# adaLN projections of a two-layer backbone: row tiles summed on VectorE, the rows of a tile on TensorE

## The chip, the cores and the metric

The kernel runs on one core of a Trainium2 chip. The metric is the device time of one execution in microseconds (us), lower is better. The engines named below are TensorE (PE in the views; PEld is its weight load), VectorE (DVE), ScalarE (ACT), GpSimd (POOL) and SyncE (SP), whose queue issues the large loads in order.

## The reference

A backbone of two layers with 1024 features works on 512 tokens: 256 of a context and 256 latents. Each layer has a mixer (attention, a Fourier branch and a recurrence, gated and merged) and an FFN with a convolution. Both are modulated by six chunks of 1024 columns, a product of a conditioning vector with `w_ada` and a bias: one vector for the latents, one for the context.

```python
silu_c = jax.nn.silu(c)
silu_cc = jax.nn.silu(c_ctx)
for l in range(DEPTH):
    mx = jnp.split((silu_c @ w_ada[l] + b_ada[l])[:, None, :], N_MOD, axis=-1)
    mc = jnp.split(silu_cc @ w_ada[l] + b_ada[l], N_MOD, axis=-1)
    hx = modulate(rms_norm(x, norm_mix[l]), mx[0], mx[1])
    hc = modulate(rms_norm(ctx, norm_mix[l]), mc[0], mc[1])
    ...
    x = x + mx[2] * y_x
    x = x + mx[5] * conv_ffn(modulate(rms_norm(x, norm_ffn[l]), mx[3], mx[4]), ...)
    if not last:
        ...
        ctx = ctx + mc[2] * y_c
        ctx = ctx + mc[5] * conv_ffn(modulate(rms_norm(ctx, norm_ffn[l]), mc[3], mc[4]), ...)
```

`w_ada` has 1024 rows and 6144 columns per layer, 24 MB in fp32. The last layer's context is read by its attention, so chunks 0 and 1 are needed there for both streams; chunks 2 to 5 only for the latents.

## The kernel before

Tokens lie feature-major. Every large product is split in three fp32r matmuls (`gemm`, recorded at L129): high times high, high times low, low times high. Weights come in loads of up to 1 MB: `chunk` (L164) issues them on SyncE into one of three `raw` buffers. A unit of weights is then split: `wh` is a rounded copy (L151 on ScalarE, or L153 on VectorE where `wmode["hi"]` says so, as in both layers' branches) and `wl` the rest (L158 on VectorE). There are three `wh` and three `wl` buffers. A usual load feeds two units, a unit feeds 24 matmuls.

The program runs through: a start with the first adaLN block in quarters (`ada_quarter`), layer 0's attention (70 to 176 us), its branches and output (to 512), its FFN (to 890), layer 1's attention (to 1004) and branches (to 1147), and the rest of layer 1. These are rough bounds, read from the trace.

The other five adaLN blocks, of two chunks each (2048 columns), are made by `ada_steps`. A step loads 128 rows of a block and multiplies: the stationary operand is `cvec`, 128 rows by 32 columns of which two hold the two conditioning vectors, the moving one 512 columns of weights. Four such matmuls fill four strips of 32 partitions of one bank, `pa`, and eight steps add up in it. Then VectorE copies the bank out (`adar`, L361), four transposes (`pt`, L364) bring the features onto partitions, and two adds (L368) put the bias on.

`ada_steps` is a generator whose steps are put between other work: `emit` takes so many steps at once, `spread` takes a fraction of a step with each later load of weights. Layer 0's blocks 1 and 2 go at two steps per head into its attention, layer 1's block 0 into layer 0's FFN, layer 1's blocks 1 and 2 into its attention (one step per head) and branches. A scheduler orders each engine's instructions from there; loads keep the program's order.

The fp32 `pa` matmuls have two records each in the trace. Tiles are named in the views: `sc`, `pt` (L832) and `pv` are the attention's scores, transposes and weighted values, `pr` its probabilities, `proj`, `gt`, `out`, `down` the large products, `uf`, `fa`, `ff` the Fourier features, `y`, `sg`, `ri` and `av` tiles of the recurrence and the merge.

## Time and profile before

| | |
|---|---|
| runs | 1417.83, 1414.15, 1417.03 us, median 1417.03 |
| span of the profiled execution | 1416.0 us |
| TensorE busy | 1374.2 us (97%) |
| VectorE busy | 892.9 us (63%) |
| ScalarE busy | 668.8 us (47%) |
| GpSimd busy | 231.9 us (16%) |
| read from HBM | 193.02 MB, 137 GB/s over the span |

The profile is of one execution. Its span runs from the first to the last instruction, and the runs' median stands 1.0 us above it. Busy shares are means over the whole span; the stretches differ, and the windows below tell them apart. The chain that ended last is followed back from the last instruction, at each step to what released it.

### The profile page before, as it was taken

To read this page: it belongs to the slowest core of one execution; us is meant where nothing else is said; L and a number is where in the kernel's file an instruction comes from. 1 tells how busy PE (TensorE), PEld (TensorE's weight loads), DVE (VectorE), ACT (ScalarE), POOL (GpSimd) and SP (SyncE) were. 2 spreads that over 40 slices of the span, in tenths; PEclk is the share of its full clock that TensorE was granted. 3 is DMA by queue.
4 is the path that set the end of the run, shared out by engine and by line. 5 is a ranking of instruction groups with operands and counts; after the bars stand their busy time and mean duration, and the time that the engine had idled before them with its cause. 6 is when DMAs were issued, how large, how long until landed. Compare 5 with 4: busy or idle time off the path is not lost.

```text
span 1416.0 us, 20938 instructions
## 1 busy us (share of the span) xinstructions
PE 1374.2 (97%) x8362; PEld 1172.5 (83%) x8362; DVE 892.9 (63%) x1451; ACT 668.8 (47%) x1136; POOL 231.9 (16%) x223
## 2 busy tenths in 40 slices
PE   7999999999999999999999999999999999999997
PEld 5676598888888898888888887878688899999997
DVE  3687648667634565555443543687788986777575
ACT  5575635423532444344322433475355665566454
POOL 2021013113200101211100111010122431122012
PEclk9999999999999999999999999999999999999999
DMA  9433715233233502222343337225465666455643
GB/s 332 135 107 131 272 35 170 80 97 100 79 100 110 172 31 90 86 96 87 89 123 120 104 116 245 62 80 191 152 219 183 197 190 199 135 194 175 196 140 100
DMA packets 187777, 195.41 MB, mean 138 GB/s; under 512 B 9340, under 2 KB 178290, under 8 KB 182560
## 3 DMA queue, kind: packets, MB, share of 16 engines
q1 hardware_dynamic: 186624, 193.23, 42.6%
q8 instruction: 65, 1.06, 0.3%
q0 software_dynamic: 1056, 0.86, 0.2%
q14 instruction: 32, 0.26, 0.1%
HBM read 193.02 MB, written 1.05 MB: 137 GB/s over the span
## 4 chain that ended last, share of the span: by engine, by line
PE 85%; DVE 7%; DMA 3%; ACT 2%; issue 2%; SPq 0%; POOL 0%; ACTq 0%; DVEq 0%; POOLq 0%
PE proj L129 49%; PE down L129 8%; PE out L129 7%; PE lat L129 4%; PE pa L129 3%; PE uf L129 2%; PE sc L129 2%; PE pv L129 2%; PE gt L129 2%; DVE wl L158 2%; PE pt L832 1%; DVE wh L153 1%; DMA raw<-in_w_in_dram 1%; DMA raw<-in_w_ada_dram 1%; PE kn L129 1%
## 5 line engine op out<-in xcount | busy, mean ns | idle before, releaser
L158 DVE TENSOR_TENSOR wl<-raw,wh 128x1024 fp32r<-128x1024 f32 (+9 forms) x339 | 339.4, 1014 | 160.8 <-ACT wh L151 156.1
L129 PE MATMUL proj<-hh,wh 128*128 128x512 f32 (+1 forms) x1232 | 417.8, 340 | 5.5 <-DVE sg L989 2.2
L129 PE MATMUL proj<-hh,wl 128*128 128x512 f32 (+1 forms) x1232 | 416.9, 339 | 0.2 <-DVE wl L158 0.2
L129 PE MATMUL proj<-hl,wh 128*128 128x512 f32 (+1 forms) x1232 | 416.8, 339 | 0.0
L151 ACT CAST wh<-raw 128x1024 fp32r<-128x1024 f32 (+7 forms) x275 | 216.3, 808 | 264.0 <-PE proj L129 153.9
L129 PEld LDWEIGHTS proj<-hh,wh 128*128 128x128 f32 x1232 | 236.1, 192 | 31.9 <-issue 3.1
L129 PEld LDWEIGHTS proj<-hh,wl 128*128 128x128 f32 x1232 | 236.1, 192 | 25.3 <-DVE wl L158 0.7
L129 PEld LDWEIGHTS proj<-hl,wh 128*128 128x128 f32 x1232 | 236.0, 192 | 24.5
L1181 POOL TENSOR_TENSOR gate<-gate,up 128x512 f32<-128x512 f32 (+1 forms) x44 | 55.3, 1257 | 445.4 <-ACT gate L1180 424.7
L153 DVE CAST wh<-raw 128x1024 fp32r<-128x1024 f32 x64 | 54.4, 853 | 52.7 <-PE proj L129 46.4
L129 PE MATMUL down<-gTh,wh 128*128 128x512 f32 (+1 forms) x224 | 75.5, 337 | 0.0
L129 PE MATMUL down<-gTh,wl 128*128 128x512 f32 (+1 forms) x224 | 75.4, 337 | 0.0
L129 PE MATMUL down<-gTl,wh 128*128 128x512 f32 (+1 forms) x224 | 75.3, 336 | 0.0
L158 DVE TENSOR_TENSOR gTl<-gate,gTh 128x512 fp32r<-128x512 f32 (+1 forms) x44 | 24.6, 559 | 78.5 <-ACT gTh L151 78.5
L129 PE MATMUL pa<-raw,cvec 128*32 128x512 f32 (+1 forms) x576 | 62.7, 457 | 3.9 <-DMA raw<-in_w_ada_dram 3.8
L442 POOL TENSOR_TENSOR sq<-sq,sq 128x256 f32<-128x256 f32 (+1 forms) x28 | 31.6, 1129 | 198.6 <-ACT sq L440 197.0
L1070 DVE SCALAR_TENSOR_TENSOR xr<-out,ada,xr 128x256 f32<-128x256 f32 x48 | 22.2, 480 | 44.1 <-PE out L129 44.1
L129 PE MATMUL out<-mh,wl 128*128 128x256 f32 (+1 forms) x152 | 47.4, 312 | 0.0
L129 PE MATMUL out<-mh,wh 128*128 128x256 f32 (+1 forms) x152 | 47.4, 313 | 0.0
L129 PE MATMUL out<-ml,wh 128*128 128x256 f32 (+1 forms) x152 | 47.4, 312 | 0.0
L151 ACT CAST gTh<-gate 128x512 fp32r<-128x512 f32 (+1 forms) x44 | 22.6, 514 | 51.3 <-POOL gate L1181 51.3
L129 PEld LDWEIGHTS down<-gTh,wh 128*128 128x128 f32 x224 | 42.5, 190 | 4.4
(287 smaller groups left out, 2725.3 us busy)
## 6 DMA issues: line engine op xcount, KB each, us to landing
raw<-in_w_up_dram SPq DMA_DIRECT2D x44, 1024.0 KB, 5.0
raw<-in_w_ada_dram SPq DMA_DIRECT2D x40, 1024.0 KB, 4.9
raw<-in_w_in_dram SPq DMA_DIRECT2D x30, 1024.0 KB, 5.3
raw<-in_w_down_dram SPq DMA_DIRECT2D x16, 896.0 KB, 5.2
raw<-in_w_ada_dram SPq DMA_DIRECT2D x32, 256.0 KB, 7.5
raw<-in_w_in_dram SPq DMA_DIRECT2D x16, 512.0 KB, 4.9
raw<-in_w_out_dram SPq DMA_DIRECT2D x8, 1024.0 KB, 5.3
raw<-in_w_down_dram SPq DMA_DIRECT2D x16, 512.0 KB, 3.8
```

Of the source, the lines that this page charges most:

```text
L129: pinned(nc.tensor.matmul(o, lhsT, rhs, start=start, stop=stop))
L151: nc.scalar.copy(out, in_)
L153: eng.tensor_copy(out, in_)
L158: (lo_eng or nc.vector).tensor_tensor(lo, src, hi, op=ALU.subtract)
L442: eng.tensor_tensor(self.terms[0][:, r], self.terms[0][:, r], sq[:, r], op=ALU.add)
L832: nc.tensor.transpose(o[:, c], probs[i][:, kt * P : (kt + 1) * P], ident)
L1070: nc.vector.scalar_tensor_tensor(xr[m][:, r], o[:, y], gate[:, s, m : m + 1], xr[m][:, r], op0=ALU.mult, op1=ALU.add)
L1181: nc.gpsimd.tensor_tensor(g, g, us[z], op=ALU.mult)
```

## The change

The five blocks are cut into 16 jobs. A job loads half tiles of 512 rows by 512 columns (1 MB, four row tiles of 128). VectorE multiplies each row tile by its 128 values of the conditioning vector, a scalar per partition, and adds it to an accumulator 128x512: one TENSOR_SCALAR and seven SCALAR_TENSOR_TENSOR for each of two accumulators. TensorE then sums over the 128 partitions with a stationary block of ones, four strips of 256 columns; ScalarE copies the sums (`adar`), two transposes and four small adds follow. `ada_both` is a job of 512 columns for both streams (two loads), `ada_latent` one of 1024 columns for the latents alone (four loads). Layer 0 has eight `ada_both`; layer 1 has four, and four `ada_latent` for chunks 2 to 5, whose context columns are filled with zeros. There are 40 loads of 1 MB as before.

Where they stand changes too. Layer 0's attention takes one step per pair of heads, its branches the rest of layer 0's jobs, layer 0's FFN all of layer 1's; layer 1's mixer has none. In layer 0's branches the `wh` copies go from VectorE to ScalarE. The accumulators share slots with other tiles, but have two buffers each of their own in layer 0's FFN. Of the diff, removed comments and the end of the old `ada_steps` are left out:

```diff
-    def ada_steps(l, blk, col, res, tag="raw"):
-        pa = bank("pa", "e")
-        for k in range(8):
-            v = chunk(a["w_ada"][l][k * P : (k + 1) * P, blk * 2048 : (blk + 1) * 2048].unsqueeze(1), 1, 2048, tag)
-            for j in range(4):
-                mm(pa[32 * j : 32 * j + 32, :], cvec[:, k, :], v[:, 0, 512 * j : 512 * (j + 1)], k == 0, k == 7)
-            if k < 7:
+    def ada_steps(l, jobs):
+
+        cols = columns_of[l]
+
+        def fetch(job, i):
+            c0, half = job[0][i]
+            src = a["w_ada"][l][half * 512 : (half + 1) * 512, c0 : c0 + 512]
+            return chunk(src.rearrange("(k p) c -> p k c", p=P), 4, 512)
+
+        def summed(quarters, two):
+            pa = bank("pa", "e")
+            for g, (z, o, *_) in enumerate(quarters):
+                mm(pa[32 * g : 32 * g + 32, 0:256], ones[:, 0:32], two[z][:, o : o + 256], True, True)
+            rows = slot("adar", "s", F32)
+            nc.scalar.copy(rows[:, 0:256], pa[:, 0:256])
+            return quarters, pa, rows
+
+        def spread_out(quarters, pa, rows):
+            for u in range(2):
+                nc.tensor.transpose(pa[:, 256 + u * P : 256 + (u + 1) * P], rows[:, u * P : (u + 1) * P], ident)
+            view = pa[:, 256:512].rearrange("p (u r) -> p r u", u=2)
+            for g, (z, o, s, j) in enumerate(quarters):
+                blk, f = j // 16, j % 16
+                nc.vector.tensor_tensor(
+                    adas[l][blk][:, s, f : f + 2], view[:, 32 * g], cols["b_ada"][:, j : j + 2], op=ALU.add
+                )
+
+        sums = None
+        for n, job in enumerate(jobs):
+            halves, quarters, todo = job
+            v = fetch(job, 0)
+            yield
+            if sums:
+                spread_out(*sums)
+            accs = [slot("acc", t, F32) for t in ("aa", "ab")]
+            for i, (c0, half) in enumerate(halves):
+                after = fetch(job, i + 1) if i + 1 < len(halves) else None
+                for k in range(4):
+                    for z, s in todo[i]:
+                        w, sc = v[:, k, :], cvec[:, 4 * half + k, s : s + 1]
+                        if half == 0 and k == 0:
+                            nc.vector.tensor_scalar(accs[z], w, sc, None, op0=ALU.mult)
+                        else:
+                            nc.vector.scalar_tensor_tensor(accs[z], w, sc, accs[z], op0=ALU.mult, op1=ALU.add)
+                    if k == 1 and len(todo[i]) > 1:
+                        yield
+                v = after
                 yield
-        rows = slot("adar", "s", F32)
-        nc.vector.tensor_copy(rows, pa)
...
+            sums = summed(quarters, accs)
+        yield
+        spread_out(*sums)
         yield
+    def ada_both(chunk_of, part):
+
+        c0 = chunk_of * D + part * 512
+        quarters = [(s, o, s, (c0 + o) // P) for s in range(2) for o in (0, 256)]
+        return ((c0, 0), (c0, 1)), quarters, [[(0, 0), (1, 1)]] * 2
+
+    def ada_latent(chunk_of):
+
+        c0 = chunk_of * D
+        quarters = [(z, o, 1, (c0 + z * 512 + o) // P) for z in range(2) for o in (0, 256)]
+        return (
+            tuple((c0 + z * 512, half) for z in range(2) for half in range(2)),
+            quarters,
+            [[(z, 1)] for z in range(2) for _ in range(2)],
+        )
...
-                    emit(steps, 1 if last else 2)
+                    if not last and e == 1:
+                        emit(steps, 1)
...
-                    wmode["hi"] = [nc.vector]
-                    if last:
-                        spread(steps, 0.5)
+                    wmode["hi"] = [nc.vector] if last else [nc.scalar]
+                    if not last:
+                        emit(steps, 1)
+                        spread(steps, 1.6)
...
-            spread(steps, 0.4)
+            spread(steps, 1.6)
...
-        with phase("ffn", gT=32, c=8), banks(dict(out="mm"), mm=5, rb=2):
+        with phase("ffn", gT=32, c=8, **({} if last else dict(aa=2, ab=2))), banks(dict(out="mm"), mm=5, rb=2):
...
+    for b in range(1, 3):
+        nc.gpsimd.memset(adas[1][b], 0.0)
+    parts_of = lambda chunks: [ada_both(c, part) for c in chunks for part in range(2)]
...
-        0, columns_of[0], adas[0], False, h, first_tiles, chain(par0, ada(0, 1), ada(0, 2)), sq_ffn,
+        0, columns_of[0], adas[0], False, h, first_tiles, chain(par0, ada_steps(0, parts_of((2, 3, 4, 5)))), sq_ffn,
...
-    steps = chain(iter([None] * 3), params(1, nc.gpsimd), final_gains(), ada(1, 0))
+    steps = chain(
+        params(1, nc.gpsimd), final_gains(),
+        ada_steps(1, parts_of((0, 1)) + [ada_latent(c) for c in range(2, 6)]),
+    )
...
-    steps_mix = chain(ada(1, 1), ada(1, 2))
...
-        1, columns_of[1], adas[1], True, h_mix, lambda half: None, steps_mix, sq_ffn,
+        1, columns_of[1], adas[1], True, h_mix, lambda half: None, iter(()), sq_ffn,
```

On TensorE, in layer 0's attention before, a chunk's four matmuls stand between the attention's own (`pv` weighted values, `pt` transposes, `sc` scores):

```order
L129 MATMUL pv_1889<-ptl_1867,vh_1379 64x256
L129 MATMUL pv_1889<-pth_1866,vl_1380 64x256
L129 MATMUL pa_1830<-raw_1943,cvec 32x512
L832 MATMUL pt_1920<-ident,pr_1843 128x128
L832 MATMUL pt_1920<-ident,pr_1855 128x128
L832 MATMUL pt_1920<-ident,pr_1843 128x128
L832 MATMUL pt_1920<-ident,pr_1855 128x128
...
L129 MATMUL pv_1889<-ptl_1876,vh_1399 64x256
L129 MATMUL pv_1889<-pth_1875,vl_1400 64x256
L129 MATMUL pa_1830<-raw_1943,cvec 32x512 x3
L129 MATMUL pa_1830<-raw_1949,cvec 32x512 x4
L129 MATMUL sc_1955<-kh_779,qh_1687 128x256
```

In the changed kernel, at the end of the first job there:

```order
L129 MATMUL pv_2006<-ptl_1971,vh_1337 64x256
L129 MATMUL pv_2006<-pth_1970,vl_1338 64x256
L129 MATMUL pa_2654<-acc_1882,ones 32x256
L129 MATMUL pv_2006<-pth_1993,vh_1337 64x256
L129 MATMUL pa_2654<-acc_1882,ones 32x256
L129 MATMUL pa_2654<-acc_1883,ones 32x256 x2
L882 MATMUL pt_1997<-ident,pr_1947 128x128
L882 MATMUL pt_1997<-ident,pr_1959 128x128
...
L129 MATMUL pv_2006<-pth_1993,vl_1338 64x256
L373 MATMUL pa_2654<-ident,adar_2659 128x128
L129 MATMUL pv_2006<-pth_2002,vh_1357 64x256
L373 MATMUL pa_2654<-ident,adar_2659 128x128
```

Before, each load brought four matmuls of 512 columns from `raw`; now a job of two loads brings four of 256 columns and two transposes, and the sums read `acc`, which VectorE's multiply-adds write.

On VectorE, in layer 0's FFN before, between three splits of weights `wl` there is only the convolution's work (`up`):

```order
L158 TENSOR_TENSOR wl_5381<-raw_5339,wh_5380 128x1024
L1116 SCALAR_TENSOR_TENSOR up_5302<-proj_5277,cols_678,up_5302 128x2x255
L1119 SCALAR_TENSOR_TENSOR up_5302<-proj_5277,cols_682,up_5302 128x2x255
L158 TENSOR_TENSOR wl_5422<-raw_5419,wh_5421 128x1024
L1116 SCALAR_TENSOR_TENSOR up_5335<-proj_5310,cols_678,up_5335 128x2x255
L1119 SCALAR_TENSOR_TENSOR up_5335<-proj_5310,cols_682,up_5335 128x2x255
L158 TENSOR_TENSOR wl_5455<-raw_5419,wh_5454 128x1024
```

In the changed kernel, the same kind of place:

```order
L158 TENSOR_TENSOR wl_5638<-raw_5596,wh_5637 128x1024
L1168 SCALAR_TENSOR_TENSOR up_5551<-proj_5526,cols_680,up_5551 128x2x255
L397 SCALAR_TENSOR_TENSOR acc_5763<-raw_5755,cvec,acc_5763 128x512
L1171 SCALAR_TENSOR_TENSOR up_5551<-proj_5526,cols_684,up_5551 128x2x255
L397 SCALAR_TENSOR_TENSOR acc_5764<-raw_5755,cvec,acc_5764 128x512
L397 SCALAR_TENSOR_TENSOR acc_5763<-raw_5755,cvec,acc_5763 128x512
L397 SCALAR_TENSOR_TENSOR acc_5764<-raw_5755,cvec,acc_5764 128x512
L158 TENSOR_TENSOR wl_5683<-raw_5680,wh_5682 128x1024
```

Four multiply-adds of a job have come between two splits.

On SyncE before, from the last heads of layer 1's attention into its branches:

```order
L164 DMA raw_8624<-in_w_in_dram 128x8x256
L164 DMA raw_8705<-in_w_ada_dram 128x2048
L164 DMA raw_8768<-in_w_ada_dram 128x2048
L164 DMA raw_8809<-in_w_ada_dram 128x2048
L164 DMA raw_8830<-in_w_ada_dram 128x2048
L164 DMA raw_8856<-in_dft_l_dram 128x2x256
L164 DMA raw_8866<-in_dft_c_dram 128x256
L912 DMA raw_8963<-in_w_in_dram 128x8x128 x2
...
L164 DMA raw_9100<-in_w_in_dram 128x8x256
L164 DMA raw_9165<-in_w_ada_dram 128x2048
```

In the changed kernel:

```order
L164 DMA raw_8896<-in_w_uq_dram 128x3x192
L164 DMA raw_9003<-in_w_in_dram 128x8x256
L164 DMA raw_9202<-in_dft_l_dram 128x2x256
L164 DMA raw_9212<-in_dft_c_dram 128x256
L963 DMA raw_9309<-in_w_in_dram 128x8x128 x2
...
L164 DMA raw_9446<-in_w_in_dram 128x8x256
L164 DMA raw_9510<-in_w_o_fourier_dram 128x4x256
```

The loads of `w_ada` among the gate weights (`w_in`) of layer 1 are gone from here; 14 stand in layer 0's branches and 24 in its FFN instead, 2 are left in its attention.

## Rows read from the trace of the kernel before

**Rows 1.** The page, parts 1 and 4: busy time of the engines; shares of the chain.

```profile
PE 1374.2 (97%) x8362; PEld 1172.5 (83%) x8362; DVE 892.9 (63%) x1451; ACT 668.8 (47%) x1136; POOL 231.9 (16%) x223
...
PE 85%; DVE 7%; DMA 3%; ACT 2%; issue 2%; SPq 0%; POOL 0%; ACTq 0%; DVEq 0%; POOLq 0%
```

**Rows 2.** Windows: stretch, length, busy PE, PEld, DVE, ACT, POOL, PEclk, DMA share, GB/s.

```profile
70.00:176.00 106.00, 103.00 (x620) 71.41 (x620) 79.00 (x201) 69.13 (x171) 13.61 (x11) 0.98 0.48 171
85.00:113.00 28.00, 27.01 (x154) 21.63 (x152) 26.65 (x75) 22.70 (x58) 6.55 (x5) 1.00 0.25 92
205.00:465.00 260.00, 260.00 (x1175) 214.68 (x1174) 161.01 (x190) 103.68 (x136) 53.45 (x44) 1.00 0.34 105
512.00:890.00 378.00, 375.38 (x1793) 308.89 (x1793) 188.37 (x277) 142.51 (x192) 44.14 (x43) 1.00 0.36 112
930.00:1004.00 74.00, 73.79 (x482) 55.92 (x480) 54.57 (x120) 42.88 (x104) 7.63 (x10) 0.98 0.40 135
1004.00:1147.00 143.00, 134.66 (x930) 117.49 (x925) 123.65 (x155) 80.51 (x112) 44.69 (x38) 0.98 0.61 192
```

**Rows 3.** Windows of tile `pa` alone: stretch, length, busy PE, PEld, DVE, ACT, then PEclk, DMA.

```profile
70.00:176.00 106.00, 22.52 (x120) 4.02 (x120) 0.69 (x1) 0.00 (x0) 0.98 0.48 171
205.00:465.00 260.00, 1.07 (x8) 0.16 (x8) 0.69 (x1) 0.00 (x0) 1.00 0.34 105
512.00:890.00 378.00, 8.31 (x64) 1.36 (x64) 0.69 (x1) 0.00 (x0) 1.00 0.36 112
930.00:1004.00 74.00, 13.24 (x64) 1.92 (x64) 0.00 (x0) 0.00 (x0) 0.98 0.40 135
1004.00:1147.00 143.00, 8.99 (x70) 1.26 (x64) 1.36 (x2) 0.00 (x0) 0.98 0.61 192
```

**Rows 4.** Chain that ended last, by line, from 115 to 176 and from 930 to 1004.

```profile
by line: PE pa L129 31.9%; PE pv L129 24.3%; PE sc L129 18.3%; PE pt L832 13.3%; PE proj L129 7.1%; PE kn L129 2.3%; DVE atl L158 1.1%; PE pt L364 0.9%; DVE nmx L813 0.7%; issue 0.3%
...
by line: PE pa L129 16.7%; PE sc L129 16.0%; PE uf L129 15.7%; PE pv L129 14.6%; PE pt L832 10.6%; PE proj L129 8.7%; PE kn L129 8.5%; PE v L129 4.1%; ACT kh L151 1.6%; ACT wh L151 1.4%; ACT pr L816 0.9%; DVE kl L158 0.9%; DVE nl L158 0.5%;
```

**Rows 5.** Pieces of that chain in order of time: start, length, what, its records.

```profile
27.99 1.88 PE pa L129 x64
...
115.97 1.85 PE pa L129 x16
...
122.82 0.97 PE pa L129 x2
...
150.11 0.56 PE pt L364 x4
...
512.69 165.11 PE proj L129 x766
...
1004.52 3.87 DMA raw<-in_w_in_dram
...
1104.58 3.98 DMA raw<-in_w_in_dram
```

**Rows 6.** VectorE's groups by form: count, busy time, mean ns, idle before and its releaser.

```profile
L153 DVE CAST wh<-raw 128x1024 fp32r<-128x1024 f32 x64 | 54.4, 853 | 52.7 <-PE proj L129 46.4 <-DMA raw<-in_w_in_dram 5.6 <-PE uf L129 0.6
...
L820 DVE TENSOR_SCALAR pr<-pr,rs 128x512 f32<-128x512 f32 x24 | 11.7, 486 | 0.3
...
L949 DVE SCALAR_TENSOR_TENSOR ri<-a,ri 128x512 f32<-128x512 f32 x16 | 11.4, 730 | 0.0
...
L995 DVE TENSOR_TENSOR sg<-sg,sg 128x512 f32<-128x512 f32 x8 | 5.5, 691 | 0.2
...
L965 DVE TENSOR_TENSOR y<-y,gug 128x512 f32<-128x512 f32 x4 | 4.9, 1228 | 2.3 <-POOL y L964 2.3
...
L368 DVE TENSOR_TENSOR ada<-pt,cols 128x16 f32<-128x16 f32 x10 | 1.2, 166 | 1.3 <-PE pt L364 1.3
```

**Rows 7.** SyncE's waits from 925 to 1150: waited for, us, times, longest.

```profile
SPq L164 <- DVE wl L158: 82.4, 18, 19.6
SPq L164 <- PE pa L129: 70.1, 14, 9.8
```

**Rows 8.** The page, part 6: loads of `w_up` weights, KB each, us to landing.

```profile
raw<-in_w_up_dram SPq DMA_DIRECT2D x44, 1024.0 KB, 5.0
```

More of the change, by code (lines that the diff above doesn't have):

```diff
@@ L85, in slot @@
     def slot(s, tag="n", dtype=F32R, w=512):
-        pool, bufs = where[tag]
+        pool, bufs, tag = where[tag]
         return pool.tile([P, w], dtype, tag=tag, name=nm(s), bufs=bufs)
@@ L96, in phase @@
             was = {t: where.get(t) for t in tags}
-            where.update({t: (pool, n) for t, n in tags.items()})
+            where.update({t: (pool, n, t) for t, n in tags.items()})
             yield
@@ L215, in backbone @@
     ctx.enter_context(phase("all", h=16, n=3, s=2, acc=1, raw=3))
+    where.update(aa=where["s"], ab=where["acc"])
     ctx.enter_context(banks(dict(ss="e"), e=1))
@@ L349, in params @@
         yield
-    def ada_steps(l, blk, col, res, tag="raw"):
-        pa = bank("pa", "e")
-        for k in range(8):
-            v = chunk(a["w_ada"][l][k * P : (k + 1) * P, blk * 2048 : (blk + 1) * 2048].unsqueeze(1), 1, 2048, tag)
-            for j in range(4):
-                mm(pa[32 * j : 32 * j + 32, :], cvec[:, k, :], v[:, 0, 512 * j : 512 * (j + 1)], k == 0, k == 7)
-            if k < 7:
-                yield
-        rows = slot("adar", "s", F32)
-        nc.vector.tensor_copy(rows, pa)
-        pt = bank("pt", "e")
-        for q in range(4):
-            nc.tensor.transpose(pt[:, q * P : (q + 1) * P], rows[:, q * P : (q + 1) * P], ident)
-        view = pt.rearrange("p (q j r) -> p j q r", q=4, r=32)
-        bias = col["b_ada"][:, blk * 16 : (blk + 1) * 16].rearrange("p (j q) -> p j q", q=4)
-        for s in range(2):
-            nc.vector.tensor_tensor(
-                res[:, s, :].rearrange("p (j q) -> p j q", q=4), view[:, :, :, s], bias, op=ALU.add
-            )
-        yield
+    def ada_steps(l, jobs):
[40 more added lines that the diff above has]
+                v = after
+                yield
+            sums = summed(quarters, accs)
+        yield
+        spread_out(*sums)
+        yield
@@ L1207, in backbone @@
     adas = [[par.tile([P, 2, 16], F32, tag=f"ada{b}", name=nm("ada")) for b in range(3)] for _ in range(DEPTH)]
-    ada = lambda l, b: ada_steps(l, b, columns_of[l], adas[l][b])
+    for b in range(1, 3):
+        nc.gpsimd.memset(adas[1][b], 0.0)
+    parts_of = lambda chunks: [ada_both(c, part) for c in chunks for part in range(2)]
     def latent_banks():
```

## The prediction, made before the changed kernel ran

> **What bounds the kernel now.** I read the page first, then windows over stretches of the program, then the adaLN sums inside those windows, then the pieces of the chain that ended last. The page shows TensorE busy for 97% of a span of 1416.0 us, and 85% of the chain on it [rows 1]. So what counts is work on TensorE, and the gaps in it. The windows say where something else is near [rows 2]. In layer 0's branches (205 to 465) and its FFN (512 to 890) TensorE has no gap to speak of, and VectorE is busy for 161.0 of 260 us (62%) and 188.4 of 378 us (50%). In layer 0's attention (70 to 176) VectorE has 79.0 of 106 us, and 26.65 of 28 us (95%) in its densest part (85 to 113): there the two engines share the bound. Layer 1's attention (930 to 1004) has TensorE at 73.8 of 74 us, VectorE at 54.6. In layer 1's branches (1004 to 1147) TensorE has 8 us of gaps and VectorE is at 86%. The granted clock is 0.98 to 1.00 in all of these, the upper of its two levels (2.4 GHz), so no term below is a clock term.
>
> The adaLN sums, tile `pa`, take 22.5 us of TensorE in layer 0's attention, 8.3 in the FFN, 13.2 and 9.0 in layer 1's attention and branches, and 1.1 in layer 0's branches [rows 3]: 54 us. They are on the chain, not beside it: `pa` is 31.9% of the chain from 115 to 176 (19.5 us), its first line, and 16.7% of that from 930 to 1004 (12.4 us), its first line again [rows 4].
>
> **The change part by part.** An fp32 matmul has two records, so a piece of 16 is two chunks of four strips: 1.85 us, or 0.93 us for a chunk; alone a chunk shows 0.97, and four transposes 0.56. The narrow sums at the start, 128 columns, take 1.88 us for eight groups of four strips, 0.235 each [rows 5].
>
> One new job on TensorE: a group of four strips of 256 columns was never run before. It lies between 0.235 and 0.93; a straight line through the two gives 0.47, and I take 0.5. Two transposes are half of 0.56. So 0.78 us a job, 12.5 us for 16 jobs against the 54 us and the 20 old transposes (2.8 us): 44 us less TensorE work.
>
> One new job on VectorE: 14 multiply-adds of 128x512 with two inputs in SBUF and a per-partition scalar. The operation is in the trace with that form, 730 ns (L949); a TENSOR_SCALAR of that size takes 486 (L820), and four small adds at 166 (L368) 0.66 us [rows 6]. 14 x 0.73 + 2 x 0.486 + 0.66 = 11.9 us a job, 190 us in all. Off VectorE go 32 casts of `wh` at 853 ns in layer 0's branches (27 us, to ScalarE, which has 103.7 of 260 us there [rows 2] and so hides them), and five copies and ten adds (5 us). The 16 copies of 256 columns of the new sums go to ScalarE too, and two fills of zeros to GpSimd at the start: nothing for either. The page's VectorE total goes from 893 to about 1050 us: still under TensorE as a whole, so the stretches decide.
>
> *Layer 0's attention* (106 us). TensorE loses 22.5 us and gets one job, 0.8: a floor of 84. VectorE gets one job and loses a copy: 79.0 + 11.9 - 0.7 = 90. It has not run above 95% of a stretch here [rows 2], which makes 95 us: **-11**. Bounds: -22, if the job falls in VectorE's own gaps; -6, if VectorE reaches only 90% (100 us). The order of this stretch shows the four sums standing directly behind the job's last multiply-adds, with nothing between: a wait of some tenths, inside these bounds.
>
> *Layer 0's branches* (260 us). Seven jobs: 7 x 0.78 = 5.5 on TensorE, less the old 1.1 and four transposes of 0.56: +4. VectorE: 161 - 27 + 7 x 11.9 = 217 us, 83%. What TensorE eats here is split weights, 24 matmuls of 0.2155 us (165.11 us for 766 [rows 5]), 5.2 us a unit, with three units of buffer. The order puts up to 15 multiply-adds between two splits, 11 us, which two units in hand (10.4 us) do not quite cover. I take +2 for that: **+6**. Bounds: +4, nothing seen; +18, if each of seven jobs costs 2 us.
>
> *Layer 0's FFN* (378 us). Off: 8.3 and 0.56; on: eight jobs, 6.2; and +1 for waits: **-2**. VectorE goes to 188 + 95 = 283 us, 75%, and no two splits have more than six multiply-adds (4.4 us) between them in the order, less than one unit of TensorE. Bounds: -3; +10, if a job costs 1.5 us of waiting.
>
> *Layer 1's attention* (74 us). 12.4 us of chain go, nothing comes. VectorE's 54.6 us would be 89% of the 61.6 left: **-12**. Bounds: -12.4; -6, where VectorE's waits come up.
>
> *Layer 1's branches* (143 us). The chain's own pieces are one chunk (1.0), a copy (0.7) and transposes (0.6). Two waits for weights, 3.87 and 3.98 us, stand in it too [rows 5], and SyncE waited 70.1 us in 14 pieces for `pa` before it could issue its next load [rows 7]: the queue is in order, so a gate weight stands behind adaLN loads that wait for a raw buffer. After, no adaLN load is left in this queue. The waits then go in part, as 18 other waits are for `wl`; and VectorE, at 86%, limits what the rest gives: of 10 us I take **-8**. Bounds: -2, the chain's own pieces alone; -18, all of `pa` (9.0 and 1.4) and both waits.
>
> The loads are 40 of 1 MB as before. 38 of them now stand among the weights of layer 0's branches (14) and FFN (24, before 8). They add 14 and 16 MB to stretches that moved 105 and 112 GB/s at a DMA share of 0.34 and 0.36, which makes 0.52 and 0.50: below the 0.61 of layer 1's branches [rows 2]. I put nothing down for bandwidth. What hides them is the three raw buffers: a transfer lands in 5.0 us [rows 8], half the 10.3 us that TensorE has from a 1 MB chunk of weights (two units).
>
> Sum: -11 + 6 - 2 - 12 - 8 = -27, so a span of 1389. The runs' median, 1417.03, is 1.0 above the profiled span; with that, **1390 us**. All good bounds together give 1416 - 22 + 4 - 3 - 12.4 - 18 = 1365, all bad ones 1416 - 6 + 18 + 10 - 6 - 2 = 1430.
>
> **A rule that speaks against it.** Two like operations show a spread: `y`<-`y,gug` 128x512 released by GpSimd, which goes on with its next work, took 1228 ns, `sg`<-`sg,sg` 128x512 took 691 [rows 6]. GpSimd is busy for 53.45 of 260 us in layer 0's branches [rows 2], 21%; if each of the 98 multiply-adds there met it at that rate and lost 0.54 us, that is 11 us of VectorE: 228 us, 88% of 260. The Trainium skill, "SBUF — State Buffer", section "Who interferes with whom", says that a VectorE instruction with two SBUF inputs contends with a GpSimd one that reads SBUF, as its second input comes through a shared interface. By that rule every multiply-add of this change is of the exposed kind, which would put these 11 us on VectorE in full; by the row of the very operation, 730 ns and so 39 ns over the 691, it is 4 us, and these stand in the sum already. The rest, 7 us of an engine at 83%, would cost nothing where TensorE has units in hand, and 1397 us in all where it has not.
>
> **The rivals.** *VectorE becomes the bound in layer 0's branches and FFN.* For: 83% and bursts of up to 15 operations; the contention above makes 88%. Against: TensorE has three units in hand, and 50% in the FFN leaves room. At the bad bounds of both stretches, 12 us each above what I took, the time is 1390 + 24 = 1414, and with half of that 1402: it lands at 1400 to 1414.
>
> *Larger gain.* Attention at its TensorE floor and layer 1's branches freed of all `pa` and both waits: 1390 - 11 - 10 = 1369, down to 1366. For: the 70 us of SyncE; against: VectorE at 86% and 95%.
>
> *Slower: weights arrive late in layer 0.* An adaLN tile now keeps one of three raw buffers until eight multiply-adds are done, not four matmuls: 5.8 us of VectorE and what is queued between them, and the weights behind it on SyncE wait that long. That is a mechanism seen in layer 1's branches [rows 7]. It decides from 27 / 38 = 0.7 us a load in branches and FFN; at 1.5 us each it is 57 us, or 1447. Against: a load takes 5.0 us to land of the 10.3 that it feeds TensorE [rows 8].
>
> *No change in effect*: the sums were hidden after all, 1417. Against: their share of the chain [rows 4].
>
> **How the numbers follow.** Forecast 0.60, VectorE as bound 0.17 (of which 0.03 ends within 0.3% of before), larger gain 0.13, late weights 0.07, no effect 0.03. A measurement of this kernel can tell about 0.3%, 4.2 us: faster is below 1412.8, slower above 1421.3. Faster: 0.60 + 0.13 + 0.14 = 0.87; same 0.06; slower 0.07. The range leaves out 0.07 above for late weights, 0.03 for no effect and the upper part of the VectorE case, and little below: 1366 to 1410.
>
> **What would show it.** Right: `pa` gone from 930 to 1147, 64 sums of 256 columns near 0.12 us each, multiply-adds near 0.73 us, layer 0's attention 95 us long with VectorE at 95%, SyncE's waits for `pa` gone, layer 0's branches longer by 6 us with VectorE at 83%. Wrong: multiply-adds at 0.9 us or more; TensorE's gaps before `wh`, `wl` in layer 0's branches or FFN; DMA pieces in the chain there; layer 1's branches as long as before, held by VectorE alone.

## The result: 0.6% slower, and the profile after

The changed kernel takes 1424.82 us (median of four runs, 1422.04 to 1425.65) against 1415.62 us of the kernel before on the same chips (four runs): a ratio of 1.0059, 95% interval 1.0044 to 1.0074 (the quotient of the two medians is 1.0065). The forecast was 1390, and its range ended at 1410. The profiled execution is that of 1422.04 us; its span is 1420.2, 4.2 us above that of the kernel before, where the medians differ by 9.2: the profiled run is the fastest of its four, that of the kernel before the slowest of its four. The other three runs, 1424.05 to 1425.65, have no trace; their mean granted clock is 0.980 to 0.982, that of the profiled run 0.984. What follows from the traces accounts for the 4.2 us.

The page of the changed kernel, the rows that answer to [rows 1]:

```profile
PE 1348.2 (95%) x8182; PEld 1169.2 (82%) x8182; DVE 1038.4 (73%) x1724; ACT 720.2 (51%) x1197; POOL 238.6 (17%) x225
...
PE 69%; DVE 17%; ACT 6%; DMA 4%; issue 3%; POOL 1%; SPq 0%; ACTq 0%; DVEq 0%; POOLq 0%
```

TensorE lost 26 us of busy time, but its share of the chain fell from 85% to 69%: VectorE has 17% of it in place of 7%, ScalarE 6% in place of 2%. Work was taken off the engine that bounds the kernel, and waits came in.

To see where, I cut both traces at the same matmuls: the first into `uf` (end of layer 0's attention), the first `out<-mh` (its branches done), the first `out<-gTh` (its FFN done), the last into `pv` (layer 1's attention done) and the last `out<-mh` (layer 1's mixer done). The rows by tile give the first and last start of a group. Before:

```profile
L129 PE MATMUL uf<-wh,hh x96: 277/283/387, 176.0 to 989.0; 128*128 128x256 f32 x96
L129 PE MATMUL out<-mh,wh x152: 277/283/499, 462.5 to 1206.5; 128*128 128x256 f32 x112, 128*128 128x512 f32 x40
L129 PE MATMUL out<-gTh,wh x104: 277/283/499, 833.8 to 1407.4; 128*128 128x256 f32 x64, 128*128 128x512 f32 x40
L129 PE MATMUL pv<-pth,vl x80: 276/277/362, 95.8 to 1004.9; 128*64 128x256 f32 x80
```

The same of the changed kernel:

```profile
L129 PE MATMUL uf<-wh,hh x96: 278/283/387, 165.5 to 992.3; 128*128 128x256 f32 x96
L129 PE MATMUL out<-mh,wh x152: 278/283/389, 473.5 to 1210.5; 128*128 128x256 f32 x112, 128*128 128x512 f32 x40
L129 PE MATMUL out<-gTh,wh x104: 277/283/499, 849.4 to 1411.5; 128*128 128x256 f32 x64, 128*128 128x512 f32 x40
L129 PE MATMUL pv<-pth,vl x80: 274/278/285, 96.6 to 1004.5; 128*64 128x256 f32 x80
```

The differences of these starts are the lengths of the stages, here for all kernels of the study (us, profiled executions; e1 to e12 are told below). The last column is the ratio to the kernel before on the same chips; the quotient of the medians can differ from it by some 0.1%.

| kernel | attention 0 | branches 0 | output and FFN 0 | to end of attention 1 | branches and output 1 | rest | ratio, 95% |
|---|---|---|---|---|---|---|---|
| before | 176.0 | 286.5 | 371.3 | 171.1 | 201.6 | 209.5 | 1 |
| changed | 165.5 | 308.0 | 375.9 | 155.1 | 206.0 | 209.7 | 1.0059 (1.0044 to 1.0074) |
| e1 casts back | 164.6 | 316.9 | 377.4 | 154.8 | 207.0 | 209.6 | 1.0106 (1.0087 to 1.0124) |
| e2 no loads | 172.7 | 305.4 | 377.3 | 157.1 | 207.1 | 209.7 | 1.0095 (1.0072 to 1.0117) |
| e3 loads only | 162.3 | 294.8 | 377.2 | 154.9 | 204.0 | 209.8 | 0.9937 (0.9915 to 0.9960) |
| e4 layer 1 only | 179.1 | 286.5 | 376.5 | 155.9 | 205.5 | 209.8 | 0.9979 (0.9966 to 0.9992) |
| e5 idle sums | 165.5 | 308.2 | 375.9 | 161.9 | 205.9 | 212.8 | 1.0087 (1.0069 to 1.0104) |
| e6 block 2 on TensorE | 179.3 | 286.4 | 374.8 | 155.2 | 198.0 | 209.6 | 0.9906 (0.9888 to 0.9924) |
| e7 half of layer 0 | 172.3 | 296.7 | 375.9 | 154.9 | 206.2 | 209.8 | 1.0007 (0.9996 to 1.0019) |
| e8 layer 0 moved, TensorE | 165.2 | 304.8 | 375.9 | 155.0 | 207.1 | 209.6 | 0.9995 (0.9983 to 1.0007) |
| e9 idle sums in place | 164.7 | 309.6 | 377.4 | 155.1 | 200.3 | 213.5 | 1.0000 (0.9987 to 1.0012) |
| e10 zeros later | 177.3 | 286.7 | 376.2 | 156.4 | 199.4 | 209.9 | 0.9906 (0.9890 to 0.9922) |
| e11 finer steps | 165.9 | 300.4 | 374.1 | 159.0 | 204.2 | 209.8 | 0.9978 (0.9959 to 0.9996) |
| e12 TensorE in the FFN | 177.2 | 286.5 | 379.4 | 168.3 | 199.5 | 209.0 | 1.0024 (1.0009 to 1.0039) |

In the changed kernel attention 0 gained 10.5 us and attention 1 16.0; branches 0 lost 21.5, the FFN 4.6 and branches 1 4.4. Two places are far from the forecast: branches 0 and branches 1. (The last stage but one runs on to 1206.5, so it holds the mixer's output too, beside the branches that the prediction ends at 1147.)

Windows over these two stages, before (columns as in [rows 2]):

```profile
176.00:462.50 286.50, 286.50 (x1404) 241.52 (x1401) 172.00 (x206) 110.11 (x150) 53.45 (x44) 1.00 0.32 98
1004.90:1206.50 201.60, 193.26 (x1416) 176.30 (x1415) 165.28 (x214) 110.78 (x158) 58.25 (x48) 0.98 0.61 195
```

And of the changed kernel:

```profile
165.50:473.50 308.00, 298.83 (x1464) 242.93 (x1463) 223.61 (x313) 154.82 (x198) 55.79 (x44) 0.99 0.44 138
1004.50:1210.50 206.00, 187.00 (x1345) 177.49 (x1343) 163.43 (x207) 116.44 (x163) 58.70 (x48) 0.96 0.48 145
```

In branches 0 VectorE's busy time rose by 52 us (56 were forecast) and is 73% of the stage: by the mean it is no bound. Yet TensorE, without a gap before, now has 9 us of them. What it waits for, from 190 to 475 (waiting engine, for what: us, times, longest):

```profile
PEld proj L129 <- DVE wl L158: 10.2, 11, 2.6
PE proj L129 <- DVE wl L158: 5.9, 7, 2.2
PEld proj L129 <- ACT wh L151: 2.9, 4, 1.1
```

These are the splits of weights, on VectorE: 10.2 us for the weight loads and 5.9 for the matmuls, two lists that overlap, beside 9.2 us of gaps in TensorE's busy time. The chain from 240 to 400, by line, shows what stands ahead of them, the multiply-adds (L397):

```profile
by line: PE proj L129 23.0%; DVE acc L397 16.7%; issue 7.4%; DVE wl L158 6.8%; DMA raw<-in_w_in_dram 6.7%; DVE ri L1005 3.5%; ACT L1032 3.2%; ACT L995 3.2%; ACT ri L988 2.9%; ACT wh L151 2.6%; DVE ri L1010 2.4%; DVE acc L395 2.4%; POOL y L1
```

SyncE's waits from 165 to 475 show the other candidate, buffers held by the multiply-adds, with transfers in the chain above (6.7%):

```profile
SPq L164 <- DVE wl L158: 84.8, 22, 12.9
SPq L164 <- DVE acc L397: 63.1, 12, 24.1
...
SPq L963 <- DVE acc L397: 12.2, 2, 8.0
```

In branches 1 VectorE does the same work as before less 1.9 us, TensorE has 6 us less, no adaLN load is left, and the stage is 4.4 us longer. Two things differ. One is the granted clock, 0.96 in place of 0.98. The other is ScalarE, with 5 instructions and 5.7 us more: loads of its tables between activations of different kinds. Those at the sigmoid of the gates (`sg`) in this stage, before and in the changed kernel:

```profile
L981 ACT ACT_TABLE_LOAD x8 | 10.3, 1283 | 0.1
```

```profile
L1032 ACT ACT_TABLE_LOAD x12 | 15.4, 1283 | 5.7 <-PE proj L129 5.5
```

In all there are 28 such loads in the stage before and 33 in the changed kernel, 1283 ns each: without the sums on TensorE, ScalarE's order is another one too.

### The profile page after: what moved, and what is told of

It reads as the page before. It is cut to its first block, busy times and chain, and to the rows that moved or that the text cites. A ratio compares the mean times of both kernels' runs of the same rounds, so it can differ in the third digit from the quotient of the medians.

```text
span 1420.2 us, 20935 instructions
## 1 busy us (share of the span) xinstructions
PE 1348.2 (95%) x8182; PEld 1169.2 (82%) x8182; DVE 1038.4 (73%) x1724; ACT 720.2 (51%) x1197; POOL 238.6 (17%) x225
## 4 chain that ended last, share of the span: by engine, by line
PE 69%; DVE 17%; ACT 6%; DMA 4%; issue 3%; POOL 1%; SPq 0%; ACTq 0%; DVEq 0%; POOLq 0%
PE proj L129 39%; PE down L129 8%; PE out L129 8%; PE lat L129 4%; DVE wl L158 3%; DMA raw<-in_w_in_dram 3%; DVE acc L397 2%; PE uf L129 2%; ACT wh L151 1%; PE gt L129 1%; PE sc L129 1%; PE pt L882 1%; PE pa L129 1%; PE pv L129 1%; DVE wh L153 1%
## 5 line engine op out<-in xcount | busy, mean ns | idle before, releaser
L151 ACT CAST wh<-raw 128x1024 fp32r<-128x1024 f32 (+8 forms) x307 | 249.1, 833 | 289.7 <-PE proj L129 126.9
L129 PEld LDWEIGHTS proj<-hh,wl 128*128 128x128 f32 x1232 | 237.2, 193 | 34.8 <-DVE wl L158 10.2
L397 DVE SCALAR_TENSOR_TENSOR acc<-raw,cvec,acc 128x512 f32<-128x512 f32 x224 | 172.9, 804 | 6.6 <-DMA raw<-in_w_ada_dram 5.3
L1233 POOL TENSOR_TENSOR gate<-gate,up 128x512 f32<-128x512 f32 (+1 forms) x44 | 59.6, 1354 | 456.8 <-ACT gate L1232 403.8
L1232 ACT ACTIVATE gate<-gate 128x512 f32<-128x512 f32 (+1 forms) x44 | 23.1, 524 | 53.9 <-DVE gate L1171 53.6
L129 PEld LDWEIGHTS down<-gTh,wl 128*128 128x128 f32 x224 | 42.5, 190 | 4.4
```

The source lines that it names most:

```text
L129: pinned(nc.tensor.matmul(o, lhsT, rhs, start=start, stop=stop))
L151: nc.scalar.copy(out, in_)
L397: nc.vector.scalar_tensor_tensor(accs[z], w, sc, accs[z], op0=ALU.mult, op1=ALU.add)
L1232: nc.scalar.activation(g, g, AF.Gelu_apprx_tanh)
L1233: nc.gpsimd.tensor_tensor(g, g, us[z], op=ALU.mult)
```

## The experiments

Theory A: in branches 0 weights come late, since an adaLN tile holds a raw buffer until its multiply-adds are done. Theory B: VectorE's own time there, queued ahead of the splits, makes TensorE wait. Theory C: the casts moved to ScalarE queue behind its activations. For branches 1: the clock falls when TensorE's sums are gone, against order and work of the other engines alone.

**e1, casts back on VectorE.**

```diff
-                    wmode["hi"] = [nc.vector] if last else [nc.scalar]
+                    wmode["hi"] = [nc.vector]
```

> The changed kernel with the 32 wh casts of layer 0's branches back on VectorE. Theory A (weights of layer 0's branches come late: an adaLN tile keeps one of three raw buffers until its multiply-adds, queued on VectorE, are done, and the weights stand behind it on SyncE): the hold grows with VectorE's queue, 0 to +6 us against the changed kernel. Theory B (VectorE's own time, 27 us more of it ahead of the splits): +10 us or more. Theory C (the moved casts queue behind ScalarE's activations): -10 us or more, down to 1415 or less.

Branches 0 took 316.9 us, 8.9 more than in the changed kernel; the median is 1431.59. C is out: moving the casts to ScalarE had helped. The stage lies between A (up to 6 us) and B (10 or more) and doesn't tell them apart.

**e2, no loads.** The multiply-adds stay in count and shape.

```diff
-            c0, half = job[0][i]
-            src = a["w_ada"][l][half * 512 : (half + 1) * 512, c0 : c0 + 512]
-            return chunk(src.rearrange("(k p) c -> p k c", p=P), 4, 512)
+            return xr[7]
...
-                        w, sc = v[:, k, :], cvec[:, 4 * half + k, s : s + 1]
+                        w, sc = v, eps
```

> The changed kernel without the 40 adaLN loads: the multiply-adds, same count and shape, read a resident tile and a constant scalar, so the modulation's values are not the reference's. Theory A: layer 0's branches back from 285 us to about 268, the whole about 1400. Theories B and C: VectorE and ScalarE do all that they did, so the branches stay within 4 us of 285 and the whole stays at 1418 to 1425.

**e3, loads only.**

```diff
-                        else:
-                            nc.vector.scalar_tensor_tensor(accs[z], w, sc, accs[z], op0=ALU.mult, op1=ALU.add)
+                        elif k == 3:
+                            nc.vector.scalar_tensor_tensor(
+                                accs[z][:, 0:32], w[:, 0:32], sc, accs[z][:, 0:32], op0=ALU.mult, op1=ALU.add
+                            )
```

> The changed kernel with its 40 loads, sums and transposes, but most multiply-adds left out: of 14 a job 10 are gone and 4 work on 32 columns, so the modulation is wrong. Theory A: a tile is released almost as it lands, about 1398 to 1404, like the kernel without loads. Theory B: the same gain, as VectorE is free. Theory C: no gain from it in layer 0's branches, 1418 or more. If the transfers themselves are in the way (order and bandwidth), the branches keep 10 us or more of their loss here.

Without loads the kernel is no faster (1429.84, above what any of the theories had put down), and branches 0 are 305.4 us in place of 308.0. Without most multiply-adds it is 1406.66 (A and B had 1398 to 1404), and branches 0 are 294.8, so 8.3 us of their loss stay. The windows of branches 0 in e2 and e3:

```profile
190.00:478.00 288.00, 279.54 (x1319) 226.13 (x1319) 206.44 (x285) 147.87 (x186) 56.85 (x44) 0.99 0.31 93
```

```profile
180.00:457.00 277.00, 275.77 (x1316) 225.02 (x1315) 151.72 (x231) 148.60 (x186) 51.67 (x44) 1.00 0.48 150
```

And what TensorE waited for in e2, from 190 to 478:

```profile
PEld proj L129 <- DVE wl L158: 8.6, 5, 2.6
PE proj L129 <- DVE wl L158: 6.6, 5, 2.2
```

The same 15 us of waits for `wl` with no adaLN load in the queues at all, and 8.5 us of gaps in TensorE; with all the loads and 152 us of VectorE, gaps of 1.2 us. A falls as the main cause, B stands: 13.2 of the 21.5 us in branches 0 go with the multiply-adds (308.0 against 294.8). 8.0 of them are gaps of TensorE that close (9.2 to 1.2 us over the stage); the other 5.3 are less busy time for the same matmuls, part of it from the clock (1.00 in place of 0.99). In e2 the scheduler also placed the multiply-adds differently: 100 in place of 112 are in branches 0, 12 more in attention 0, which lost 7 us against the changed kernel. So the 2.6 us are not the loads' alone, and why the whole grew stays open.

**e4, layer 1 only.** Layer 0 goes back to the old code (`emit(steps, 2)` in its attention, casts on VectorE, the old `ada_steps`).

```diff
-        0, columns_of[0], adas[0], False, h, first_tiles, chain(par0, ada_steps(0, parts_of((2, 3, 4, 5)))), sq_ffn,
+        0, columns_of[0], adas[0], False, h, first_tiles, chain(par0, ada(0, 1), ada(0, 2)), sq_ffn,
```

> Layer 0's blocks as in the kernel before (sums in its attention on TensorE, casts on VectorE), layer 1's as in the changed kernel. All theories put the loss of 21 us in layer 0's branches on the jobs there and the gain of 10 us in its attention on their leaving: without both, 1416 + 5 (layer 0's FFN) - 16 (to the end of layer 1's attention) + 4 (layer 1's branches), about 1409. If the loss in layer 1's branches depends on layer 0, less than 1405.

1413.69, a ratio of 0.9979, where about 1409 was expected. Branches 0 are at 286.5 again, and branches 1 at 205.5: their loss is layer 1's own. Attention 0 is 3 us longer than before (179.1), most of what the expectation missed.

**e5, idle sums in branches 1.** Eight groups of matmuls of a resident tile.

```diff
+    def idle_sums():
+        for k in range(8):
+            o = bank("idle", "e")
+            for j in range(4):
+                nc.tensor.matmul(o[32 * j : 32 * j + 32, :], cvec[:, k, :], xr[7], start=True, stop=True)
+            yield
...
+                    else:
+                        spread(idle_sums(), 0.5)
```

> The changed kernel, with eight groups of four 512-column matmuls of a resident tile, whose sums nothing reads, put back among layer 1's branches on TensorE (8 us of it, no loads). Clock theory (TensorE's clock falls to 0.81 there because it idles more once its adaLN sums are gone): clock 0.98 or more through layer 1's branches, that stage 3 us or more shorter than the 206 us of the changed kernel, the whole 1419 to 1422. Rival (VectorE and its order alone set that stage): 206 to 210 us there, the whole 1425 to 1429.

Nothing follows from it: the groups depended on nothing in that stage, and the scheduler put them ahead of it. The stage to the end of attention 1 is 6.8 us longer than in the changed kernel, branches 1 unchanged (205.9), the whole 1430.36.

**e6, block 2 of layer 1 on TensorE in branches 1.** From e4:

```diff
+                    if last:
+                        spread(steps, 0.5)
...
-        ada_steps(1, parts_of((0, 1)) + [ada_latent(c) for c in range(2, 6)]),
+        ada_steps(1, parts_of((0, 1)) + [ada_latent(c) for c in range(2, 4)]),
...
-        1, columns_of[1], adas[1], True, h_mix, lambda half: None, iter(()), sq_ffn,
+        1, columns_of[1], adas[1], True, h_mix, lambda half: None, ada(1, 2), sq_ffn,
```

> Layer 0 as before, layer 1's chunks 0 to 3 on VectorE in layer 0's FFN, and chunks 4 and 5 as matmuls in layer 1's branches with their eight loads. If TensorE's sums there are free, in gaps, and keep its clock: branches of layer 1 at 201 to 202 us as before, two jobs less in the FFN, 1408 to 1410. If the eight loads among the gate weights cost what SyncE's waits looked like: 1413 or more.

1404.78, a ratio of 0.9906: faster than both kernels and than the 1408 to 1410 expected. With eight chunks more on TensorE and eight loads more among the gate weights, branches 1 are 198.0 us, 7.5 less than in e4, and the clock is 1.00:

```profile
995.70:1193.70 198.00, 189.42 (x1413) 173.36 (x1412) 163.91 (x211) 110.63 (x158) 58.31 (x48) 1.00 0.62 194
```

**e7, half of layer 0's jobs.** Chunks 2 and 3 as before in attention 0, four jobs in branches 0.

```diff
-                    if not last and e == 1:
-                        emit(steps, 1)
+                    if not last:
+                        emit(steps, 2 if p < 2 else 1 if p + e == 3 else 0)
...
-                        spread(steps, 1.6)
+                        spread(steps, 0.9)
...
+        0, columns_of[0], adas[0], False, h, first_tiles, chain(par0, ada_old(0, 1, columns_of[0], adas[0][1]), ada_steps(0, parts_of((4, 5)))), sq_ffn,
```

> The changed kernel with layer 0's chunks 2 and 3 made as before in its attention, and only four jobs (chunks 4 and 5) on VectorE in its branches, casts on ScalarE. If the loss there goes by the amount of VectorE's multiply-adds: half of 16 us of it is left, layer 0's mixer products begin at 468 us (473.5 in the changed kernel, 462.5 before), the whole about 1419. If it needs the crowding of seven jobs: 464 us, 1415.

1418.49; the mixer's products begin at 469.0 us, branches 0 are 296.7. Of the four jobs 56 multiply-adds fall into branches 0 (the other 8 into attention 0), against 112 in the changed kernel: 56 cost 10.2 us, 112 cost 21.5. The loss goes by the amount and does not need seven jobs. Fewer long bunches came with the smaller amount, so this run doesn't tell the two apart; e11 does.

**e8, layer 0's sums on TensorE, moved into branches 0.** From e4:

```diff
-                    if not last:
+                    if not last and p + e == 0:
                         emit(steps, 2)
...
+                    if not last:
+                        spread(steps, 0.75)
```

> Layer 1 as in the changed kernel; layer 0's 16 chunks summed on TensorE as before, but placed in its branches instead of its attention. If only VectorE's multiply-adds cost time there: attention 20 us shorter than before, branches 15 us longer (16 x 0.97), the whole 1407 to 1410. If the 16 loads among the branches' weights cost time by themselves: 1415 or more.

1416.90, no difference from before, and in the range put down for loads that cost time by themselves (1415 or more). Branches 0 grew by 18.3 us with TensorE busy throughout, 304.8 of 304.8 us: most of that is the sums, 15 chunks in place of 1 (16.0 us in place of 1.1; one chunk stayed in attention 0). What missed was the other stage: attention 0 gained only 10.8 us, not 20. It is 165.2 us with no VectorE job in it and 165.5 with one. Its window in e8, from 70 to 165:

```profile
70.00:165.00 95.00, 85.69 (x503) 69.70 (x504) 77.16 (x199) 69.11 (x172) 13.80 (x12) 0.95 0.14 41
```

and in the changed kernel:

```profile
70.00:165.00 95.00, 85.11 (x503) 69.01 (x504) 86.05 (x218) 69.78 (x173) 13.92 (x12) 0.96 0.18 55
```

VectorE is at 81% in one and 91% in the other, over the same length: in attention 0 VectorE's share was not what set it.

**e9, idle sums that stay in branches 1.** As e5, but their moving operand is a gate weight tile of that stage, which holds them there; nothing is loaded for them and nothing reads them.

```diff
+            if idle_left and n == 256 and kt == 8:
+                idle_left.pop()
+                o = bank("idle", "e")
+                for j in range(4):
+                    nc.tensor.matmul(
+                        o[32 * j : 32 * j + 32, :], cvec[:, 2 * j, :], v[:, 2 * j : 2 * j + 2, :], start=True, stop=True
+                    )
```

> The changed kernel, with eight groups of four 512-column matmuls among layer 1's branches whose moving operand is a gate weight tile that is there anyway, so that TensorE's order holds them in that stage; nothing reads the sums, nothing is loaded for them. Clock theory: granted clock 0.98 or more there, the stage 201 us or less in place of 206 though 8 us of TensorE are added, the whole 1417 to 1420. Rival (the eight adaLN loads, or the order of VectorE, made that stage short before): 206 us or more, the whole 1424 to 1430.

Eight us of useless TensorE work made branches 1 5.7 us shorter (200.3 in place of 206.0), and the ratio went from 1.0059 to 1.0000; the median is 1418.76. Its window:

```profile
1006.80:1207.10 200.30, 191.65 (x1409) 175.75 (x1408) 160.60 (x207) 110.73 (x158) 58.87 (x48) 0.98 0.50 150
```

In the profiled execution 3.8 us went back in the rest of the program (213.5), so its trace has no gain as a whole; it is the slowest of the ten, and the medians keep the gain. The rest is 3.1 us longer in e5 too (212.8), the other kernel with idle sums; why stays open. ScalarE's order changed along with TensorE's work: its tables are loaded 28 times in branches 1 again, as before, not 33 times. So e9 shows that TensorE's sums, without their loads, make the stage short, but not by which of the two, clock or ScalarE's order.

**e10, zeros later.** From e6, the fill of zeros moved behind layer 0's mixer.

```diff
-    for b in range(1, 3):
-        nc.gpsimd.memset(adas[1][b], 0.0)
...
+    nc.gpsimd.memset(adas[1][1], 0.0)
```

> The kernel with layer 0 as before and chunks 4 and 5 of layer 1 in its branches, with the fill of zeros moved from the start to behind layer 0's mixer. If the two early fills on GpSimd delay the start (179 us to the end of layer 0's attention in place of 176): 3 us less, 1401 to 1403. If it is the changed order of the start for another reason: 1404 to 1406.

1405.44, as e6. Attention 0 is 177.3 us, 2.0 less than in e6, but it is 177.2 in e12 below, which keeps the fills at the start: nothing shows that they cost the 1 to 3 us that attention 0 lost in e4 and e6. That small loss stays open.

**e11, finer steps.** Two multiply-adds to a step, handed out by weight unit in branches 0.

```diff
-                    if k == 1 and len(todo[i]) > 1:
+                    if k < 3:
...
-                        spread(steps, 1.6)
+                        spread(steps, 1.5)
+                        by_unit[:], ticks[:] = list(ticks), []
...
-            spread(steps, 1.6)
+            spread(steps, 2.9)
```

> The changed kernel with steps of two multiply-adds instead of four to eight, handed out by weight unit in layer 0's branches and more of them per load in its FFN: no more than 10 between two splits (12 to 15 before), the same number in all. If bursts make TensorE wait: layer 0's branches 300 us or less in place of 308, the whole 1417 or less. If it is the amount of VectorE's work ahead of the splits: 305 to 310, 1422 to 1427.

1414.64, a ratio of 0.9978 (at most 0.9996): with the same 112 multiply-adds in branches 0 the changed kernel is as fast as the kernel before, or a little faster. Branches 0 are 300.4 us. Their window:

```profile
166.00:466.00 300.00, 295.29 (x1461) 243.50 (x1460) 221.49 (x309) 151.91 (x196) 61.16 (x44) 0.99 0.45 142
```

VectorE's busy time there is within 2 us of the changed kernel's (221.5 and 223.6), and the most multiply-adds between two splits inside the stage went from 15 to 8: 7.6 of the 13.2 us were bunching. That the remaining 5.6 are the amount fits e7, but no run tests it alone.

**e12, placement alone.** From e6, with layer 1's blocks 0 and 1 as matmuls in the FFN.

```diff
-        ada_steps(1, parts_of((0, 1)) + [ada_latent(c) for c in range(2, 4)]),
+        ada(1, 0), ada(1, 1),
```

> Placement alone, no VectorE sums: layer 0 as before, layer 1's blocks 0 and 1 as matmuls in layer 0's FFN, block 2 as matmuls in layer 1's branches. If VectorE's sums in the FFN are nearly free and save TensorE's time: 16 chunks at 0.97 us against six jobs at 0.8, 10 to 11 us slower than the 1404.8 us of the kernel with these jobs, 1414 to 1417. If the gain of that kernel was only where the sums stand: 1404 to 1407.

1420.92, a ratio of 1.0024, 1.2% above e6. That is above the 1414 to 1417 expected. With the same placement and the same loads, VectorE's sums in layer 0's FFN are what makes e6 fast, by more than the 11 us worked out; where the rest comes from stays open.

## Why the prediction was wrong

**Branches 0, forecast +6, measured +21.5: the step that failed.** The text counted VectorE's share (83%; 73% of the longer stage) and three buffered units, and took 2 us for waits. TensorE's new work was right: a group of four strips takes 0.57 us in the chain of the changed kernel,

```profile
433.51 0.57 PE pa L129 x8
```

against 0.5 taken, so +4 net stands. The multiply-adds cost 13.2 us there (changed against e3), not 2. e2 shows that it is mainly their time on VectorE and not the transfers, which was the text's slower rival; e11 shows that 7.6 of it came from bunches of up to 15 between two splits, which the text had read in the order and put at 2 us in all, 14 at the bound. So the share of 73% said little about what VectorE delayed. The other 4 us (294.8 against 286.5 + 4) stay open: e3 keeps the loads, the first product of each accumulator and the casts on ScalarE, at a clock of 1.00.

VectorE's durations were close, the mean of the multiply-adds less so. In branches 0 they took:

```profile
L397 DVE SCALAR_TENSOR_TENSOR acc<-raw,cvec,acc 128x512 f32<-128x512 f32 x98 | 77.0, 834 | 0.2
...
L395 DVE TENSOR_SCALAR acc<-raw,cvec 128x512 f32<-128x512 f32 x14 | 8.4, 613 | 0.3 <-PE pa L129 0.3
```

The mean is 834 ns, not 730; the median is 745, and the longest took 1787. Over 691 that is 14 us for 98 of them; the estimate for meetings with GpSimd was 11, the row's 4. The rule of the Trainium skill ("SBUF — State Buffer", "Who interferes with whom") that such an operation contends with GpSimd's reads fits the long ones among them better than a flat 730 did; no run here took GpSimd's work away to show that it is the cause.

**Branches 1, forecast -8, measured +4.4: the second step that failed.** The text said that no term was a clock term, and took waits of SyncE for `pa` (70 us, of which only 36.6 lie from 1004 to 1150; the others are in attention 1) and two DMA pieces of the chain (7.85 us) for cost. In e6, with eight adaLN loads back in that queue and 33.3 us of these waits from 995 to 1140, the stage is the shortest of all, so those waits were worth nothing. What the sums did there was to keep TensorE busy, which e9 does without loads. Where the clock fell in the changed kernel:

```profile
1120.00:1147.00 27.00, 22.34 (x158) 20.86 (x157) 19.25 (x22) 18.45 (x25) 9.87 (x7) 0.94 0.39 118
1147.00:1165.00 18.00, 14.72 (x100) 14.31 (x101) 13.39 (x17) 7.84 (x12) 3.97 (x3) 0.81 0.39 117
```

TensorE was busy for 22.3 of 27 us, at 0.94, and then had a mean granted clock of 0.81 for 18 us. The levels are 1.2 and 2.4 GHz, so 0.81 is the lower one for some 38% of that time. The Trainium skill ("TensorE: Matmul & The Clock Gate", "What's actually happening") says that the lower clock is the default and that activity releases the higher one; the step from 0.96 to 0.98 with more activity in e9 agrees.

What the lower clock cost can be read from the same matmuls at either clock. Without the sums (8.5 us), the old transposes (1.3) and the idle matmuls (8.5), TensorE is busy in the stage for 183.4 us before, 187.0 in the changed kernel and 183.1 in e9. So 3.6 of the 4.4 us lost, and 3.9 of the 5.7 us that e9 gave back, are the same matmuls taking longer or less long; the rest is gaps. A step of 0.02 in the clock over 206 us is about 4 us, so the clock is enough to explain this part. In the fourteen kernels the stage follows the clock: 198.0 to 199.5 us at 0.99 and 1.00 (e6, e10, e12), 200.3 and 201.6 at 0.98 (e9, before), 204.0 and 204.2 at 0.97 (e3, e11), 205.5 to 206.2 at 0.96 (changed, e4, e5, e7), 207.0 and 207.1 at 0.94 and 0.95 (e1, e2, e8).

One rival was not tested by itself. In this stage ScalarE loads its tables 28 times in the five kernels at 0.98 and above, 31 times in e5 and 33 times in the other eight: the clock and ScalarE's order change together. Against the order alone: among the kernels with 33 loads the stage still grows by 3 us as the clock falls, and e5, with 31, has the stage and the clock of the changed kernel. For it: gaps come before a fall of the clock, and ScalarE's order may have made some of them. That the sums' leaving brought the loss is shown (e4, e6, e9); how much of it came by way of ScalarE is not.

**FFN 0 and attention 1, forecast -2 and -12, measured +4.6 and -16.0**, -11.4 together. Some of the old sums of the FFN lay behind the cut at `out<-gTh`, so only the sum of the two compares. In the first of these stages TensorE's busy time grew by 4.1 us and its gaps by 0.5, so the multiply-adds cost next to nothing there, as forecast. Right in mechanism, 2.6 us too good in size.

**Attention 0, forecast -11, measured -10.5.** The size was right and the reason was not: VectorE at 95% was to set it, but e8 gives the same length with VectorE at 81%. What does set it stays open; the granted clock of 0.95 to 0.96 there may be one part.

Of the rivals, VectorE as bound in branches 0 came nearest. Its bad bound for that stage, +18, was 3.5 us short, and the loss in the other stage, which no rival had, came on top. Of the text's own signs of being wrong, two came: gaps of TensorE before `wl` in branches 0, and DMA pieces in the chain there (6.7%).

## What to carry to other kernels

An engine that is busy for 73% of a stage did delay a consumer with three buffered units here: price work put ahead of a producer by what TensorE would wait at the worst bunch, and hand it out in the smallest steps. The same sums were worth moving in a stage where VectorE was at half (the FFN, e6 against e12) and not where it was at 60% with bunches. And before taking TensorE work out of a stage in which TensorE already waits for others, look at its granted clock there: in branches 1 that work was free, and its removal cost time.

## What the runs showed of the hardware

Eight us of matmuls that nothing reads shortened a stage of 206 us by 5.7 (e9), while the granted clock rose from 0.96 to 0.98 and ScalarE's table loads (1283 ns each) went from 33 to 28; with eight real chunks (e6) the clock was 1.00 and the stage 198.0. Matmuls with ones as the stationary operand, 32x256 of fp32, took 0.57 us for a group of four strips, close to the 0.5 interpolated between 0.235 and 0.93 [rows 5].
